# The MLP's second product: its seventh Strassen product by seven inner products as well, and its combined weights made in memory

## The chip, the core and the metric

The kernel runs on one core of a Trainium2 chip. The core has five engines that run side by side, each through its own instructions in order: TensorE (PE in the profile; PEld is its weight load), VectorE (DVE), ScalarE (ACT), GpSimd (POOL) and SyncE (SP, which here only starts transfers). Matmuls write sums into PSUM, which has eight banks of 128 x 512 floats; everything else lives in SBUF, and between SBUF and the device's memory sixteen DMA engines move data. The metric is the time of one execution in microseconds on the device (us). Most executions agree within 0.3 %.

## What is computed

One layer of a diffusion backbone over 1024 tokens of width 1024: a modulated norm, a mixer (pooling beside neighbourhood attention), a residual, a second modulated norm and an MLP with a squared ReLU, a residual again. All that the change touches is the MLP and what follows it:

```python
def _sq_relu_mlp(h, w1, w2):
    return jnp.square(jax.nn.relu(h @ w1)) @ w2
...
        y_x = _sq_relu_mlp(_modulate(x, g_pre_mlp[l], sh2, sc2), w_mlp_in[l], w_mlp_out[l])
        x = x + gt2 * _rmsnorm(y_x, g_post_mlp[l])
```

h is 1024 x 1024, w1 1024 x 4096, w2 4096 x 1024, all in float32. Each operand of a product is split into a high and a low part, and a product is three matmuls (`three`, L220): high by high, high by low, low by high.

## The kernel before

**The second product.** The hidden matrix R (1024 x 4096) by w2 is done by Strassen's method in Winograd's form. R has blocks A11, A12, A21, A22 of 512 tokens by 2048, w2 has blocks b11, b12, b21, b22 of 2048 by 512. Instead of eight block products there are seven: P1 = A11·b11, P2 = A12·b21, a third one S4·b22, P6 = S2·t2, P5 = S1·t1, P7 = S3·t3, P4 = A22·t4. The S are sums of blocks of R, the t sums of blocks of w2; sums and differences of the products give the four blocks of the output. The S are made in `combine_hidden` and `combine_last` (L1981 to L1991) while the first product makes R; R and S go out to memory (`kept`) and come back as operands (`hidden`).

**Groups.** A product with 2048 inner rows is cut into eight groups g of 256 rows (`group`, L2234). A group has 24 matmuls of 512 columns: four tiles t of 128 tokens, each with a PSUM bank of its own, by two blocks of 128 rows by three parts. The four banks of P1 and P2 are called pyx, of P6 pyy, of P5 pyz, of P7 and P4 pyv. The third product is itself done by seven inner products, M1 to M7 (`INNER`, L2119), each of 256 x 1024 by 1024 x 256, in two halves h (`inner_group`, L2310): a half has 24 matmuls of 256 columns, and an inner product has one bank, called pyi. `inner_kept` adds a finished bank into pages c0, c1 (the third product), t and u. So there are 14 inner groups, placed among the groups of P1 and P2.

**Who prepares.** `items` lists all groups in PE's order. At the start of each group, `prepare` (L2169) makes the operands of the item three places further (`AHEAD`): SP loads the hidden block (hrA, hrS) and the weights (b, t), ACT writes the high parts (t_5h, hhA_5h), VectorE the low parts (t_5l, hhA_5l; L175). The weights' parts lie in eight buffers, two to an item, so that those of an item wait until the matmuls of the item four places before are done. In a P6 group `operands` also makes the combined weights on VectorE: t1 = b12 − b11, t2 = t1 − b22, t3 = b22 − b12 (L2095 to L2098), writes t3 out to memory, and adds b21 to t2's page by a transfer of POOL that adds what it brings (`add_to`, L210), which makes t4.

**The order.** Within the last part of the kernel PE, ACT, VectorE and SP run in the order in which the code is written. PE's order there is P1 and P2 with the M groups, P6 and P5 in turn, P7, P4. P4's last four groups are written out another way (`late`): all four for token tile t = 0, then for t = 1, 2 and 3, so that each tile's end work (`finish`) can go on under the next tile's matmuls. In this late part a tile's bank is first made whole by VectorE: L2381 adds u2 into the banks v[t] (pyv) after P4's fourth group.

**The end of rows.** With u2 = P6 + P1 and u4 = P5 + u2, the output halves are: row t < 4, left x[t] (P1 + P2) and right c12 = third product + u4; row 4 + t, right P7 + u4 and left P7 + P4 + u2. `gated` (L2247) squares a half on ACT for the norm and multiplies it by the gate on VectorE (L2251); `finish` (L2270) does this for the second half and computes the norm's root (vy on VectorE L161, ry on POOL); `end` (L2257) multiplies by the root and adds the residual (xo, L2259), and writes the row out. In P7's groups 0 to 3 stand u4 (L2367) and c12 (L2368), in its groups 1 to 4 `finish` of rows 0 to 3, and after P7 the right halves of rows 4 to 7 (L2374).

**The first product.** It is done in 16 pairs of column blocks (`block_pair`, L1999), on the banks phx, phy, phz, phv, with w1's weights wa loaded by SP; from the eleventh pair on (`EARLY`) each pair also loads pages wmb of the modulation's weights, which VectorE sums into accb (L246). In a pair, c22 comes from the bank phv (L2020). Attention runs before, in units i = 0 to 31 (218 to 314 us); there the DMA engines have least to do.

Of the kernel before, what the change touches and what calls it, by code (L numbers as in the profile page):

```python
# [18 lines left out]
P = 128  # L19
# [84 lines left out]
def hybrid_block(ctx, tc, x, ctx_in, w_mod, mod_pages, w_u, b_mod, gp1, gp2, w_in, pool_w, rpb, w_out, w1, w2, vectors,  # L104
# [1073 lines left out]

    with (
# [128 lines left out]
        N = len(units)  # L1308

# [80 lines left out]
        with in_order(ET.PE, ET.Activation, ET.DVE, ET.SP) as projected:  # L1390
# [32 lines left out]
            for i in range(N):  # L1423
# [33 lines left out]
                if i == 2:  # L1457
                    column_sums("sc", accs["sc"], lambda name: pa[:, :256])
# [7 lines left out]
                if 1 < i < N - 1:  # L1466
# [94 lines left out]
    with tc.tile_pool(name="ps2", bufs=6, space=PSUM) as ps2:  # L1561

      def bank(name):
          if (name[:3] in ("phv", "pyi") or name in ("poz_0", "poz_1") or name[:2] == "px" and name[-2:] in ("_3", "_7")
                  or name in ("pyy_3", "pyv_3", "pyz_3")):
              return lasting(name)
          return ps2.tile([P, 512], F32, tag="mm", name=name)

      with ExitStack() as tmp2:
# [257 lines left out]
        def second_steps(b12, b22):  # L1827
# [13 lines left out]
            for name in ("T2", "T1", "T3", "B22", "T4"):  # L1841
# [9 lines left out]
                for n in ("A11", "A12", "A22", "S1", "S2", "S3")}  # L1851
        hidq = [dram.tile([P, 4, 1024], F32, tag=f"hq{h}", name=f"hq{h}") for h in range(2)]
# [49 lines left out]
        def kept(name, p):  # L1902
            if name == "S4":
                return hidq[p // 8][:, p // 2 % 4, (p % 2) * 512 : (p % 2) * 512 + 512]
# [76 lines left out]
        def combine_hidden(p, r11, r21, r22, sa, sb):  # L1981
            nc.vector.tensor_tensor(sa[:, :512], r21, r22, add)
            nc.vector.tensor_tensor(sb[:, :512], r11, r21, sub)
            nc.vector.tensor_tensor(sa[:, 512:], sa[:, :512], r11, sub)  # L1984
# [14 lines left out]
        def block_pair(p, ahead, final=False):  # L1999
# [23 lines left out]
            defer(keep, "A22", p, c22)  # L2023
            if p >= EARLY:
# [34 lines left out]
        w2v = w2.rearrange("(k i p) n -> i p k n", i=2, p=P)  # L2059
        t1, t2 = {}, {}  # L2060
# [22 lines left out]
        def operands(name, g, made=None):  # L2083
            made = made or high_low
            if name == "P1":
                t1[g] = columns(page(f"b11_{g}"), 0, 0, g)
                return hidden("A11", g, g <= AHEAD + 1), made(f"b11_{g}", t1[g])
            if name == "P2":
                return hidden("A12", g), made(f"b21_{g}", wcols("b21", 1, 0, g))
            if name in INNER:  # L2090
                return inner_operands(name, g)
            if name == "P6":

                b12, b22 = wcols("b12", 0, 1, g), wcols("b22", 1, 1, g)
                nc.vector.tensor_tensor(t1[g], b12, t1[g], sub)  # L2095
                t2[g] = page(f"t2_{g}")
                nc.vector.tensor_tensor(t2[g], t1[g], b22, sub)
                nc.vector.tensor_tensor(b12, b22, b12, sub)  # L2098
                nc.gpsimd.dma_start(t3d[g], b12)  # L2099
                parts = hidden("S2", g), high_low(f"t2_{g}", t2[g], -1.0)  # L2100
                if g < NG - 2:
                    last_added(g)
                return parts
            if name == "P5":
                return hidden("S1", g), made(f"t1_{g}", t1[g])
            if name == "P7":
                r = wraw.tile([P, 1024], F32, tag="raw", name=f"t3_{g}")
                nc.sync.dma_start(r, t3d[g])
                if g in (2, 3):
                    last_added(NG - 4 + g)  # L2110
                return hidden("S3", g), made(f"t3_{g}", r)
            return hidden("A22", g), made(f"t4_{g}", t2.pop(g))

        t3d = [dram.tile([P, 1024], F32, tag=f"t3_{g}", name=f"t3_{g}") for g in range(NG)]

        def last_added(g):
            add_to(t2[g].rearrange("p (a f) -> p a f", a=2), w2v[1][:, 2 * g : 2 * g + 2, :512])

        INNER = ("M1", "M5", "M6", "M4", "M2", "M3", "M7")  # L2119
        kept_raw, combine = {}, nc.vector.tensor_tensor  # L2120

        def inner_raw(name, left, r, c, h, at=None):
            if at is None:
                at = tmp.tile([P, 1024], F32, tag="h", name=name, bufs=4) if left else wraw.tile([P, 1024], F32, tag="raw", name=name)
            nc.sync.dma_start(at.rearrange("p (a f) -> p a f", a=4),
                              hidq[h][:, :, c * 512 + r * 256 : c * 512 + r * 256 + 256] if left else
# [315 lines left out]
```

## Time and profile before

| | us |
|---|---|
| median of 3 runs | 1017.34 (1017.3 to 1017.37) |
| the profiled execution | 1017.39 |
| its span in the trace | 1015.6 |
| first product of the second matrix starts (pyx) | 706.9 |
| P6 and P5 start | 835.3 |
| P7 starts | 922.3 |
| P4 starts | 965.9 |

A view of the profile called a timeline has one row for each instruction: start, duration, engine, line, operation, out<-in, and in brackets how long the engine had sat idle before it and what it waited for. Windows give each engine's busy time in a stretch, and the share of the sixteen DMA engines that is taken. Durations overlap a little on a pipelined engine (a matmul of 0.39 us is followed by the next after 0.23), so costs are taken from start to start.

### The profile page before, as it was taken

How to read it: one execution, taken by the hardware profiler on the slowest of the kernel's cores; microseconds unless marked ns; L12 is line 12 of the kernel's file. 1: busy time of each engine (PE TensorE's matmuls, PEld its weight loads, DVE VectorE, ACT ScalarE, POOL GpSimd, SP SyncE). 2: the span in 40 equal slices, each digit the busy share in tenths (PEclk: the TensorE clock that was granted, in tenths of full speed). 3: DMA queues.
4: the chain of work that ended last, by engine and by line, in shares of the span. 5: the costliest groups of instructions: out<-in, count | busy, mean ns of one | idle time of the engine just before them, and what ended most of it. 6: DMA issues, size and time to landing. Idle time of an engine off the chain costs nothing.

```text
span 1015.6 us, 16654 instructions
## 1 busy us (share of the span) xinstructions
PE 1005.2 (99%) x6154; PEld 839.0 (83%) x6154; DVE 772.8 (76%) x1197; ACT 558.8 (55%) x974; POOL 172.4 (17%) x254
## 2 busy tenths in 40 slices
PE   8999999999999999999999999999999999999997
PEld 5788888878998888888888888888889888888886
DVE  5588766968885789879988887755787899757763
ACT  6672254448886746786555554555555454333441
POOL 4111110166774221410000000000000011200200
PEclk9999999999999999999999999999999999999999
DMA  9899798641339945885786656536987799986532
GB/s 362 323 287 315 252 256 306 211 104 43 95 91 224 240 163 178 299 215 195 257 264 204 216 196 223 189 129 241 331 272 235 232 329 292 342 265 237 198 125 84
DMA packets 126722, 229.04 MB, mean 226 GB/s; under 512 B 9712, under 2 KB 61808, under 8 KB 126640
## 3 DMA queue, kind: packets, MB, share of 16 engines
q1 hardware_dynamic: 96240, 166.95, 48.5%
q0 software_dynamic: 13264, 30.06, 13.3%
q10 hardware_dynamic: 17136, 30.97, 8.2%
q8 instruction: 48, 0.79, 0.3%
q14 instruction: 34, 0.28, 0.1%
HBM read 170.25 MB, written 56.64 MB: 223 GB/s over the span
## 4 chain that ended last, share of the span: by engine, by line
PE 96%; DMA 2%; ACT 1%; DVE 0%; SPq 0%; issue 0%; POOL 0%; DVEq 0%; ACTq 0%
PE pu L476 4%; PE pa L1295 4%; PE S L1208 3%; PE phx L221 3%; PE pyx L221 3%; PE phz L221 3%; PE phv L221 3%; PE pyx L222 3%; PE phx L222 3%; PE phv L222 3%; PE phz L222 3%; PE phx L223 3%; PE pyx L223 3%; PE phz L223 3%; PE phv L223 3%; PE pyv L223 3%
## 5 line engine op out<-in xcount | busy, mean ns | idle before, releaser
L1899 ACT ACTIVATE c<-c 128x512 f32<-128x512 f32 x48 | 30.3, 632 | 45.8 <-DVE c L2021 27.2
L1239 ACT ACTIVATE sp<-sp,nm 128x640 f32<-128x640 f32 (+1 forms) x64 | 51.5, 804 | 6.3 <-DVE ri L1243 5.2
L1228 DVE CUSTOM_DVE_ANT_0 sp<-S,tab 128x640 f32<-128x640 f32 (+1 forms) x56 | 44.6, 796 | 13.1 <-PE pz L1261 11.3
L169 ACT CAST wpS<-S 128x512 fp32r<-128x512 f32 x64 | 38.7, 616 | 27.6 <-PE phv L223 10.1
L221 PE MATMUL phx<-thB,wpA 128*128 128x512 f32 x128 | 50.2, 392 | 0.0
L223 PE MATMUL phx<-thB,wpA 128*128 128x512 f32 x128 | 49.8, 389 | 0.0
L222 PE MATMUL phx<-tlB,wpA 128*128 128x512 f32 x128 | 49.8, 389 | 0.0
L175 DVE TENSOR_TENSOR wpS<-S,wpS 128x512 fp32r<-128x512 f32 x64 | 43.5, 687 | 8.0 <-ACT wpS L169 8.0
L1900 ACT ACTIVATE c<-c 128x512 f32<-128x512 f32 x48 | 30.3, 631 | 14.9 <-DVE sa L1984 12.1
L2099 POOL DMA_DIRECT2D t<-b x8 | 4.7, 583 | 144.6 <-DVE b L2098 144.6
L221 PEld LDWEIGHTS phx<-thB,wpA 128*128 128x128 f32 x128 | 24.0, 188 | 5.5 <-ACT s L1952 0.4
L223 PEld LDWEIGHTS phx<-thB,wpA 128*128 128x128 f32 x128 | 24.0, 188 | 5.1
L222 PEld LDWEIGHTS phx<-tlB,wpA 128*128 128x128 f32 x128 | 24.0, 188 | 4.9
L1295 PE MATMUL pa<-pt,v 128*64 128x128 f32 x352 | 25.8, 279 | 0.0
L238 POOL MEMSET accb<- 128x1024 f32 x1 | 1.0, 958 | 142.1 <-ACT c L1900 142.1
L221 PE MATMUL phz<-thB,wpS 128*128 128x512 f32 x64 | 25.0, 391 | 0.0
L221 PE MATMUL phv<-thT,wpA 128*128 128x512 f32 x64 | 25.0, 391 | 0.0
L223 PE MATMUL phz<-thB,wpS 128*128 128x512 f32 x64 | 24.9, 389 | 0.0
L223 PE MATMUL phv<-thT,wpA 128*128 128x512 f32 x64 | 24.9, 389 | 0.0
L222 PE MATMUL phv<-tlT,wpA 128*128 128x512 f32 x64 | 24.9, 389 | 0.0
L221 PE MATMUL phy<-thT,wpS 128*128 128x512 f32 x64 | 24.9, 389 | 0.0
L222 PE MATMUL phy<-tlT,wpS 128*128 128x512 f32 x64 | 24.9, 389 | 0.0
(1216 smaller groups left out, 3572.7 us busy)
## 6 DMA issues: line engine op xcount, KB each, us to landing
b<-in_w SPq DMA_DIRECT2D x32, 512.0 KB, 6.5
hrA<-hdA SPq DMA_DIRECT2D x24, 512.0 KB, 6.5
hrS<-hdS SPq DMA_DIRECT2D x24, 512.0 KB, 6.9
wm<-in_mod_pages SPq DMA_DIRECT2D x16, 512.0 KB, 9.4
wa_0w<-in_w SPq DMA_DIRECT2D x16, 512.0 KB, 4.8
wa_1w<-in_w SPq DMA_DIRECT2D x16, 512.0 KB, 4.2
hdA<-c ACTq DMA_DIRECT2D x32, 256.0 KB, 2.2
hdS<-sa ACTq DMA_DIRECT2D x32, 256.0 KB, 2.2
```

What stands on the lines that cost most here:

```text
L169: nc.scalar.copy(hi, src)
L175: nc.vector.tensor_tensor(lo, src, hi.bitcast(F32), sub)
L221: nc.tensor.matmul(ps, ahi, bhi, start=first, stop=False, skip_group_check=more)
L222: nc.tensor.matmul(ps, ahi, blo, start=False, stop=False, skip_group_check=more)
L223: nc.tensor.matmul(ps, alo, bhi, start=False, stop=last, skip_group_check=more)
L476: nc.tensor.matmul(pus[b][j], wk(wgt, k, low, j * P, P), r, start=(k == 0 and n == 0), stop=(k == KT - 1 and n == 2))
L1208: nc.tensor.matmul(S[e][:, c0 : c0 + k[0].shape[1]], q[n_q][hs, cols], k[n_k][hs], start=(n_q + n_k == 0), stop=(n_q == 1))
L1228: nc.vector.tensor_tensor_reduce(out=to, in0=s, in1=bt, scale=1.0, scalar=BIG, op0=add, op1=ALU.min, accum_out=nm)
L1239: nc.scalar.activation(sp, sp, AF.Exp, bias=least[i, e], scale=-1.0, accum_out=sums[i][:, e : e + 1])
L1295: nc.tensor.matmul(pa[e * HD : (e + 1) * HD, cols], v[:, f : f + HD], turns[i][:, e, c] if c < 4 else fifths[i][:, :, (e + 1) * HD : (e + ...
L1899: nc.scalar.activation(r, src, AF.Relu)
L1900: nc.scalar.activation(r, r, AF.Square)
```

## The change

**P7 becomes seven inner products.** `items` drops P7's eight groups; in their place fourteen inner groups N1 to N7, two halves each, stand one behind each group of P6 and P5 but for the last of either. P6's eight groups now come first, then P5's. `inner_kept` keeps the N sums in pages of their own, which together are c22 in the end part (not to be confused with the pair's c22).

**The combined weights are made in memory.** During the attention units 6 to 29, SP copies blocks of w2 within the device's memory, 24 copies of 512 KB: b22 into the places of t3 and t2, b12 into that of t1 (`block_copied`). In the pairs 2 to 14 of the first product POOL starts 24 adding transfers (`block_sums`): one in pairs 2 and 3, two in each later pair, behind a tiny copy from the pair's c22 ("pace") that keeps POOL from running ahead. POOL now runs in the written order there and to the end. In P6 and P5 the weights are then only loaded, and VectorE's three combinations are gone; t4's adding transfer moves to P5's preparation. The signs of some S are turned to fit.

**The end part.** With P7's groups gone, its work is written around P4's first four groups. u4 stands before them; in P4's group g stand c12 −= u4, `finish` of row g − 1, u2 −= c22, row 4 + g = c22 − u4, and from g = 2 on the gate of row 2 + g. After the additions into v[t] come `finish` of row 3 and the preparation of P4's last group.

The core of the diff:

```diff
+        block_copies = [(to, i, g) for g in range(4) for to, i in ((t3_page, 1), (t1_page, 0), (t2_page, 1))]
...
+        def block_copied():
+            to, i, g = block_copies.pop(0)
+            nc.sync.dma_start(to(g), w2_block(i, 1, g))
...
+                if 5 < i < 30:
+                    block_copied()
...
+        block_sums = [f for g in range(8) for f in (lambda g=g: add_to(t3_page(g), w2_block(0, 1, g)),
+                                                    lambda g=g: add_to(t1_page(g), w2_block(0, 0, g)),
+                                                    lambda g=g: add_to(t2_page(g), t1_page(g)))]
+
+        def block_summed(src, n):
+            if n:
+                pace = sm("pace_" + str(len(block_sums)), 1, 2)
+                nc.gpsimd.tensor_copy(pace, src[:, :1])
+            for _ in range(n):
+                block_sums.pop(0)()
...
             defer(keep, "A22", p, c22)
+            block_summed(c22, 0 if p < 2 or final else 1 if p < 4 else 2)
...
-                b12, b22 = wcols("b12", 0, 1, g), wcols("b22", 1, 1, g)
-                nc.vector.tensor_tensor(t1[g], b12, t1[g], sub)
                 t2[g] = page(f"t2_{g}")
-                nc.vector.tensor_tensor(t2[g], t1[g], b22, sub)
-                nc.vector.tensor_tensor(b12, b22, b12, sub)
-                nc.gpsimd.dma_start(t3d[g], b12)
-                parts = hidden("S2", g), high_low(f"t2_{g}", t2[g], -1.0)
-                if g < NG - 2:
-                    last_added(g)
+                nc.sync.dma_start(two_rows(t2[g]), t2_page(g))
+                return hidden("S2", g), high_low(f"t2_{g}", t2[g])
+            if name == "P5":
+                r = wraw.tile([P, 1024], F32, tag="raw", name=f"t1_{g}")
+                nc.sync.dma_start(two_rows(r), t1_page(g))
+                parts = hidden("S1", g), high_low(f"t1_{g}", r)
+                pace = sm(f"pace_t{g}", 1, 2)
+                nc.gpsimd.tensor_copy(pace, r[:, :1])
+                add_to(two_rows(t2[g]), w2_block(1, 0, g))
                 return parts
...
-        items += [(n, g) for g in range(NG) for n in ("P6", "P5")]
-        items += [(n, g) for n in ("P7", "P4") for g in range(NG)]
+        inner = iter([("N" + n, h) for n in INNER for h in range(2)])
+        for n in ("P6", "P5"):
+            for g in range(NG):
+                items += [(n, g), *islice(inner, 1 if g < NG - 1 else 0)]
+        assert next(inner, None) is None
+        items += [("P4", g) for g in range(NG)]
...
-            for g in range(NG):
-                group(v, "P7", g)
-                if g < 4:
-                    residual(g)
-                    nc.vector.tensor_tensor(u4[g], z[g], u2[g], add)
-                    nc.vector.tensor_tensor(c12[g], c12[g], u4[g], add)
-                if 0 < g < 5:
-                    finish(g - 1, 1, c12[g - 1], xts[g - 1])
-            end()
-            for t in range(4):
-                rows[4 + t] = page(f"row{4 + t}")
-                nc.vector.tensor_tensor(half(4 + t, 1), v[t], u4[t], add)
-            for g in range(NG // 2):
-                group(v, "P4", g, more=True, last=(g == NG // 2 - 1))
-                gated(4 + g, 1, half(4 + g, 1))
+            v, u4, c22 = four("pyv"), halves("u4"), whole("N")
+            for t in range(4):
+                residual(t)
+                nc.vector.tensor_tensor(u4[t], z[t], u2[t], add)
+            for g in range(NG // 2):
+                group(v, "P4", g, last=(g == NG // 2 - 1))
+                nc.vector.tensor_tensor(c12[g], c12[g], u4[g], sub)
+                if g > 0:
+                    finish(g - 1, 1, c12[g - 1], xts[g - 1])
+                rows[4 + g] = page(f"row{4 + g}")
+                nc.vector.tensor_tensor(u2[g], u2[g], c22[g], sub)
+                nc.vector.tensor_tensor(half(4 + g, 1), c22[g], u4[g], sub)
+                if g > 1:
+                    gated(2 + g, 1, half(2 + g, 1))
...
+            finish(3, 1, c12[3], xts[3])
             while coming:
                 prepare()
+            end()
+            for t in (2, 3):
+                gated(4 + t, 1, half(4 + t, 1))
```

What stands in a row on VectorE in P4's groups 2 and 3, up to the first addition into a bank of the late part, before (t and hhA are the low parts of weights and hidden blocks; row the right halves; pyv the bank, u the page of u2):

```order
L175 TENSOR_TENSOR t_5l<-t_5_9543,t_5h 128x1024
L2251 TENSOR_TENSOR row_10230<-row_10230,Gb 128x512
L175 TENSOR_TENSOR hhA_6l<-hrA_6_10345,hhA_6h 128x1024
L175 TENSOR_TENSOR t_6l<-t_6_9621,t_6h 128x1024
L2251 TENSOR_TENSOR row_10232<-row_10232,Gb 128x512
L2381 TENSOR_TENSOR pyv_9885<-pyv_9885,u_9842 128x512
```

and at the same place in the changed kernel, from the low part hhA_6l on (c1Mi holds c12's lower tiles, c1Ni the new c22's, s_8632 is u2's page):

```order
L175 TENSOR_TENSOR hhA_6l<-hrA_6_10622,hhA_6h 128x1024
L175 TENSOR_TENSOR t_6l<-t_6_9665,t_6h 128x1024
L2397 TENSOR_TENSOR c1Mi<-c1Mi,u_10475 128x512
L2281 SCALAR_TENSOR_TENSOR xo_10479<-c_9310,ry_10613,xo_10479 128x512
L2281 SCALAR_TENSOR_TENSOR xo_10479<-c0Mi,ry_10613,xo_10479 128x512
L161 SCALAR_TENSOR_TENSOR vy_10662<-sy_8164,sy_8165 128x1
L2271 TENSOR_TENSOR c1Mi<-c1Mi,Gb 128x512
L2401 TENSOR_TENSOR s_8632<-s_8632,c1Ni 128x512
L2402 TENSOR_TENSOR row_10667<-c1Ni,u_10475 128x512
L2271 TENSOR_TENSOR row_10568<-row_10568,Gb 128x512
L2408 TENSOR_TENSOR pyv_10470<-pyv_10470,s_8631 128x512
```

Between t_6l and the addition into the bank stood one gate; now seven 512-wide operations on data in SBUF, two of them halves of xo, and the little vy stand there. Between t_5l and hhA_6l, where one gate stood, the same list stands once more (c12, two halves of xo, vy, gate, u2, row, gate).

After that addition, VectorE's order up to the last low part, t_7l, is in the changed kernel:

```order
L2408 TENSOR_TENSOR pyv_10471<-pyv_10471,s_8631 128x512
L2408 TENSOR_TENSOR pyv_10472<-pyv_10472,s_8632 128x512
L2408 TENSOR_TENSOR pyv_10473<-pyv_10473,s_8632 128x256
L2409 TENSOR_TENSOR pyw<-pyv_10473,s_8632 128x256
L2281 SCALAR_TENSOR_TENSOR xo_10482<-c_9311,ry_10664,xo_10482 128x512
L2281 SCALAR_TENSOR_TENSOR xo_10482<-c1Mi,ry_10664,xo_10482 128x512
L161 SCALAR_TENSOR_TENSOR vy_10684<-sy_8164,sy_8165 128x1
L2271 TENSOR_TENSOR c1Mi<-c1Mi,Gb 128x512
L175 TENSOR_TENSOR hhA_7l<-hrA_7_10689,hhA_7h 128x1024
L175 TENSOR_TENSOR t_7l<-t_7_9739,t_7h 128x1024
```

Before, hhA_7l followed directly on the addition into pyw; now `finish` of row 3 (xo, vy, gate) stands between.

On POOL, around the eleventh pair of the first product, the changed kernel has the adding transfers (t2d, t3q, t1d are the places of t2, t3 and t1 in memory; c_10 is the eleventh pair's c22):

```order
L238 MEMSET accb 128x1024
L239 DMA accb<-in_b_mod 1x16x64
L2016 COPY pace_7255<-c_10_7225 128x1
L211 DMA t2d_2096<-t1d_2088 128x1024
L211 DMA t3q_2101<-in_w 128x2x512
L2016 COPY pace_7423<-c_11_7393 128x1
L211 DMA t1d_2089<-in_w 128x2x512
L211 DMA t2d_2097<-t1d_2089 128x1024
```

Before, nothing of POOL stood there but the first two rows: the two transfers behind each pace are new.

More of the change, by code (lines that the diff above doesn't have):

```diff
@@ L2055, in block_pair @@
             defer(combine_last, p, c21, sa, sb)
[L2059 to L2060 removed]
+        t2 = {}
         def columns(raw, i, h, g):
@@ L2158, in hybrid_block @@
         AHEAD = 3
-        inner = iter([(n, h) for n in INNER for h in range(2)])
+        inner = iter([("M" + n, h) for n in INNER for h in range(2)])
         items = [("P1", g) for g in range(4)]
@@ L2211, in hybrid_block @@
         fixed.append(True)
-        with tc.issue_after(first[ET.PE]), in_order(ET.PE, ET.Activation, ET.DVE, ET.SP):
+        with tc.issue_after(first[ET.PE]), in_order(ET.PE, ET.Activation, ET.DVE, ET.SP, ET.Pool):
             block_pair(NPAIR - 1, prepare, final=True)
@@ L2258, in end @@
                 for m, rs, xt in ending:
-                    nc.vector.scalar_tensor_tensor(xt, rows[m], rs, xt, mul, add)
+                    parts = [(half(m, h), xt[:, h * 512 : (h + 1) * 512]) for h in range(2)] if m < 4 else [(rows[m], xt)]
+                    for row, to in parts:
+                        nc.vector.scalar_tensor_tensor(to, row, rs, to, mul, add)
                     (nc.gpsimd if m < 4 else nc.sync).dma_start(og[m], xt)
@@ L2322, in inner_group, with whole @@
                     inner_kept(name, ps)
+            def whole(k):
+                return [parts[f"c{t // 2}{k}"][:, t % 2 * 512 : t % 2 * 512 + 512] for t in range(4)]
             x = four("pyx")
             for name, g in items[: items.index(("P6", 0))]:
-                if name in INNER:
+                if name[0] == "M":
                     inner_group(name, g)
@@ L2342, in hybrid_block @@
                         G2 = gate_page("b")
+            c12, left = whole("M"), halves("c11")
             for t in range(4):
-                rows[t] = page(f"row{t}")
+                halves_of_rows[t, 0], halves_of_rows[t, 1] = left[t], c12[t]
                 gated(t, 0, x[t])
-            y, z = four("pyy"), four("pyz")
-            for g in range(NG):
-                group(y, "P6", g)
-                if g == NG - 1:
-                    u2 = halves("u2")
-                    for t in range(4):
-                        nc.vector.tensor_tensor(u2[t], y[t], s1[t], add)
-                group(z, "P5", g)
+            y, z, u2 = four("pyy"), None, s1
+            for name, g in items[items.index(("P6", 0)) : items.index(("P4", 0))]:
+                if name[0] == "N":
+                    inner_group(name, g)
+                elif name == "P6":
+                    group(y, "P6", g)
+                    if g == NG - 1:
+                        for t in range(4):
+                            nc.vector.tensor_tensor(u2[t], s1[t], y[t], sub)
+                        z = four("pyz")
+                else:
+                    group(z, "P5", g)
             xts = {}
```

100 lines of the change are left out of this document (48 added, 52 removed).

## The prediction

> **What bounds the kernel now.** I read the page first, then the timelines of TensorE and VectorE around the products that the change touches, then the loads.
>
> ```profile
> span 1015.6 us, 16654 instructions
> ...
> PE 1005.2 (99%) x6154; PEld 839.0 (83%) x6154; DVE 772.8 (76%) x1197; ACT 558.8 (55%) x974; POOL 172.4 (17%) x254
> ...
> PEclk9999999999999999999999999999999999999999
> DMA  9899798641339945885786656536987799986532
> ...
> PE 96%; DMA 2%; ACT 1%; DVE 0%; SPq 0%; issue 0%; POOL 0%; DVEq 0%; ACTq 0%
> ```
>
> TensorE (PE) is busy 99 % of the span, the chain that ended last is 96 % PE, and the granted clock is in its top tenth in every slice. So the time is the sum of the matmuls, and an edit can act in two ways only: it shortens that sum, or it makes PE wait where it does not wait now. The profiled execution took 1017.39 us, 1.79 us more than its span; the median of the runs is 1017.34, so the sum below, made against 1017.39, can be read against the median as it stands.
>
> **What the change takes from PE.** P7's eight groups of 24 matmuls with 512 columns go; fourteen inner groups of 24 matmuls with 256 columns come. Both kinds stand in the trace (in a timeline row: start us, us, engine, line, operation, out<-in):
>
> ```profile
> 768.58 0.40 PE L221 MATMUL pyx<-b_0h,hhA_0h 128*128 128x512 f32 x1
> ...
> 774.05 0.28 PE L221 MATMUL pyiM<-wM_0h,hhM_0h 128*128 128x256 f32 x1
> ...
> 776.92 0.40 PE L221 MATMUL pyx<-b_1h,hhA_1h 128*128 128x512 f32 x1
> ...
> 927.79 0.39 PE L221 MATMUL pyv<-t_1h,hhS_1h 128*128 128x512 f32 x1
> ...
> 933.23 0.39 PE L221 MATMUL pyv<-t_2h,hhS_2h 128*128 128x512 f32 x1
> ```
>
> A P7 group takes 933.23 − 927.79 = 5.44 us (0.2267 a matmul); eight take 43.5. An inner group, from 774.05 to 776.92, takes 2.87; by the pair of slots, 776.92 − 768.58 − 5.44 = 2.90, and fourteen take 40.6. **PE saves 43.52 − 40.60 = 2.92 us.** This term is nearly sure: the same instructions ran in the same form.
>
> **What the change puts in the tail.** Before, the work that follows P7 and P5 on VectorE (u4, c12, the four rows of `finish`) was spread over P7's eight groups. Now P7 is gone as a stretch of its own, and u4, c12, `finish`, and two new subtractions per group (u2 −= c22, row = c22 − u4) all stand in P4's first four groups, between the low parts that P4 itself needs. VectorE runs in the written order, so I add up what stands there. Prices of the operations:
>
> ```profile
> 930.71 0.69 DVE L2368 TENSOR_TENSOR c0i<-c0i,u 128x512 f32<-128x512 f32 x1
> 931.32 0.15 DVE L161 SCALAR_TENSOR_TENSOR vy<-sy,sy 128x1 f32<-128x1 f32 x1
> 931.39 0.69 DVE L2251 TENSOR_TENSOR row<-c0i,Gb 128x512 f32<-128x512 f32 x1
> ...
> 936.75 1.28 DVE L2259 SCALAR_TENSOR_TENSOR xo<-row,ry,xo 128x1024 f32<-128x1024 f32 x1
> 937.95 0.15 DVE L161 SCALAR_TENSOR_TENSOR vy<-sy,sy 128x1 f32<-128x1 f32 x1
> ```
>
> From start to start a 512-wide addition costs 0.61 us, the little vy 0.07, xo 1.20. Xo now comes as two halves of 512; no row shows such a half, so I bound it by half of 1.20 (0.60) and by the 0.69 of a 512-wide row, and take 0.635. And what stands in P4 today:
>
> ```profile
> 972.37 1.23 DVE L175 TENSOR_TENSOR t_4l<-t,t_4h 128x1024 fp32r<-128x1024 f32 x1 [1.60 <-ACT t_4h L169]
> ...
> 977.81 1.23 DVE L175 TENSOR_TENSOR t_5l<-t,t_5h 128x1024 fp32r<-128x1024 f32 x1 [2.48 <-ACT t_5h L169]
> 978.95 0.69 DVE L2251 TENSOR_TENSOR row<-row,Gb 128x512 f32<-128x512 f32 x1
> 979.55 1.22 DVE L175 TENSOR_TENSOR hhA_6l<-hrA,hhA_6h 128x1024 fp32r<-128x1024 f32 x1
> 980.69 1.22 DVE L175 TENSOR_TENSOR t_6l<-t,t_6h 128x1024 fp32r<-128x1024 f32 x1
> ...
> 983.75 0.70 DVE L2381 TENSOR_TENSOR pyv<-pyv,u 128x512 f32<-128x512 f32 x1 [1.24 <-PE pyv L223]
> ...
> 987.83 0.43 DVE L2381 TENSOR_TENSOR pyv<-pyv,u 128x256 f32<-128x256 f32 x1 [0.66 <-PE pyv L223]
> 988.30 0.43 DVE L2382 TENSOR_TENSOR pyw<-pyv,u 128x256 f32<-128x256 f32 x1
> 988.64 1.22 DVE L175 TENSOR_TENSOR hhA_7l<-hrA,hhA_7h 128x1024 fp32r<-128x1024 f32 x1
> 989.77 1.22 DVE L175 TENSOR_TENSOR t_7l<-t,t_7h 128x1024 fp32r<-128x1024 f32 x1
> ```
>
> and PE's side of it:
>
> ```profile
> 965.87 0.39 PE L221 MATMUL pyv<-t_0h,hhA_0h 128*128 128x512 f32 x1
> ...
> 987.63 0.39 PE L221 MATMUL pyv<-t_4h,hhA_4h 128*128 128x512 f32 x1
> ...
> 991.93 0.39 PE L222 MATMUL pyv<-t_7l,hhA_7h 128*128 128x512 f32 x1
> ```
>
> P4 starts at T = 965.87, its first half ends 21.76 us later, at 987.63, and there PE goes on into the late products of t = 0, which first need VectorE's addition into that bank (v[0], L2381, L2408 after). Before, that addition is done at 984.45, more than 3 us early. After, t_5l can't start earlier than T + 11.94 (it waits for ACT's t_5h, which waits for a buffer that PE frees). Behind it the order of the changed kernel has, up to and with the addition for t = 0: three low parts (3 × 1.14 = 3.42), ten 512-wide operations (c12, gate row, u2, row, gate, twice: 6.05 at 0.605), four halves of xo (2.54), two vy (0.14), and the addition from PSUM (0.70): **12.85 us**, with 987.63 − 977.81 = 9.82 us of PE's work to hide in. **First wait: about 3.05 us.** What stands ahead of t_5l does not add to it: t_4l too waits for ACT, until 972.37 (T + 6.50); behind it come 1.14 of its own, c12, vy, gate, u2 and row of group 1 (2.5) and hhA_5l (1.14), done at T + 11.3, 0.65 us before t_5l can start.
>
> **Second wait.** After the addition for t = 0 stand: those for t = 1, 2 (1.26), two halves (0.81), xo (1.27), vy and gate (0.67), hhA_7l (1.14), t_7l (1.23): 6.4 us, less a tenth for the overlap of neighbours, so t_7l is done 6.3 us after that addition. PE, released by the addition, reaches t_7l after 991.93 − 987.63 = 4.30 us. **Second wait: about 2.0 us**; before, t_7l ended at 990.99, 0.94 us ahead of need. Behind it PE runs to the end as now. The tail costs 3.05 + 2.0 = 5.05 us, with bounds of 0 (all of it slides under PE) and 6.5 (a tenth more for each operation, from the row widths instead of the pitches).
>
> **What making the weights costs elsewhere.** Twenty-four plain copies of 512 KB run under attention; the DMA row above has 0.1 to 0.4 there (ninth to twelfth slice, 203 to 305 us), so I take nothing (if the copies crowded the loads behind attention, it would show as a wait of PE there). Twenty-four adding transfers run beside the MLP's first product, two to a pair of columns from the fifth pair on. Where the pairs from the eleventh on load gate weights as well, there is little room:
>
> ```profile
> 616.04 0.38 SPq L201 DMA_DIRECT2D wa_1w<-in_w  x1
> ```
> ```profile
> 623.70 0.69 DVE L1872 TENSOR_TENSOR S<-wa_0w,wa_1w 128x512 f32<-128x512 f32 x1 [3.95 <-DMA wa_1w<-in_w]
> ...
> 626.84 0.68 DVE L2020 TENSOR_TENSOR c<-phv,c 128x512 f32<-128x512 f32 x1
> ```
> ```profile
> 628.03 0.39 PE L221 MATMUL phv<-thT,wpA 128*128 128x512 f32 x1
> ```
>
> VectorE idled 3.95 us for that load (7.6 us after its issue); four operations later it read the bank phv until 627.52, and PE took that bank again at 628.03: 0.51 us of margin. What an adding transfer costs and how full the queues are (windows: us, PE busy, PEld, DVE, ACT, POOL, clock, DMA share, GB/s):
>
> ```profile
> 608.00:616.00 8.00, 8.00 (x37) 6.62 (x36) 7.76 (x11) 4.77 (x10) 0.00 (x0) 1.00 0.75 238
> 616.00:624.00 8.00, 8.00 (x37) 6.62 (x36) 4.00 (x7) 2.76 (x5) 0.00 (x0) 1.00 0.91 322
> 800.00:838.00 38.00, 38.00 (x222) 33.73 (x221) 34.90 (x33) 19.54 (x26) 3.00 (x4) 1.00 0.94 311
> 838.00:880.00 42.00, 42.00 (x187) 34.76 (x186) 35.19 (x33) 17.57 (x19) 7.78 (x9) 1.00 1.02 319
> ```
> ```profile
> q0 software_dynamic: 1794, 4.69, 43.0%
> ...
> b<-in_w SPq DMA_DIRECT2D x8, 512.0 KB, 10.1
> ...
> t<-in_w POOLq DMA_DIRECT2D x5, 512.0 KB, 9.2
> ```
>
> In 838 to 880 nine transfers of POOL's queue q0, five of them adding, took 43 % of 42 us: 2.0 us of all sixteen engines each. From 608 to 624 the share is 0.83, or 13.3 us of work in 16; two adding transfers make it 17.3, so the load lands 1.3 us late, and 0.51 of that is covered: **about 0.85 us of waiting**, once. Bounds: 0 (the adds land in the free tenth behind), and 4.5 (from 838 to 880 SP's loads of b took 10.1 us at a share of 1.02; a stall of a microsecond in each of the four or five pairs with gate weights).
>
> The Trainium skill ("DMA: Bandwidth & Descriptors", section "Issuing engines are not separate DMA queues") says that transfers issued by SP, ACT and GpSimd run on the same sixteen engines and interleave; the rows agree (1.02 and 10.1 us beside POOL's adds). If they did not share, this term would be 0 and the sum 1019.5.
>
> The stretch of P6, P5 and the new inner groups gets the density of today's P1, P2 with M groups, where PE never waited (800 to 838: 38.00 of 38.00). I take 0. VectorE loses the three combinations of each P6 group and gains the sums of the inner ones; it is not late there. The cover is thin in DMA (0.94), and if it went, each late load would cost about the 0.4 to 1 us by which it missed.
>
> **The sum.** 1017.39 − 2.92 + 3.05 + 2.0 + 0.85 = **1020.4 us**, 0.3 % slower.
>
> **Rivals.**
> - *The tail alone.* The adding transfers hide; the tail is late as worked out: 1017.39 − 2.92 + 5.05 = 1019.5. For it: the free 0.09 to 0.25 of the queues; against it: only 0.51 us of margin. 0.20.
> - *Loads late in several places.* The adds in pairs 11 to 15, and in inner groups with up to four loads of 512 KB in one slot, cost 2 to 4.5 us in place of 0.85: 1021.5 to 1024. For it: a share of 1.02 before; against it: the 38.00 of 38.00 at 0.94. 0.12.
> - *The tail fits: faster.* If VectorE gets through the stretch behind t_5l in 9.8 us in place of 12.85, the addition for t = 0 comes in time, and PE keeps its gain: 1014.5. It decides at a pitch 24 % below the rows' (or t_5l that much earlier); VectorE's idle 2.48 us before t_5l speaks for some slack, but it lies ahead of t_5l, and the stretch that decides lies behind. 0.10.
> - *Half of it.* One wait appears, the other is covered (the 0.94 us of margin, rows at their shortest): near 1017. 0.07.
> - *The clock falls in the first wait.* In the whole span PE is idle for 10.4 us (1015.6 − 1005.2), in many pieces, and the clock stands. If a wait of 3.05 us lowered the granted clock to half for as long again, the matmuls in that stretch would lose 1.5 us: 1022. The trace bears it out weakly, since the clock's row never falls: 0.06. The Trainium skill ("TensorE: Matmul & The Clock Gate", section "What's actually happening") has a free-running window of about 3.4 us after which an idle PE is halved; this trace, which shows no fall, can't say, and 3.05 us lies just below that window.
> - The forecast itself: 0.45. That the change does not do what it says has nothing for it in the orders: the 144 added matmuls and the adding transfers stand there.
>
> **Range and chances.** A difference under 0.2 % (2 us: 1015.3 to 1019.4) is about what a measurement of this kernel can't tell from none. Faster: only the tail that fits, 0.10. Same: half of the tail alone, and the half-covered case: 0.17. Slower: the rest, 0.73. The range 1015.5 to 1024.5 leaves out the fitting tail and the worst of the loads, less than 0.2.
>
> **What would show it.** In the profile of after: (1) inner groups N at 2.9 us a slot, P7's rows gone, PE's busy time lower by about 2.9; (2) VectorE without a gap from t_5l to the addition L2408, and PE waiting there for about 3 us, released by DVE; (3) a wait of about 2 us before the first matmul with t_7l, released by DVE; (4) a wait of PE near 628 us behind wa_1w. A tail without waits, or VectorE idle between P4's low parts, would prove me wrong; so would waits of PE among P6, P5 and the inner groups of more than 1 us.

## The result, and the profile after

The changed kernel took **1041.5 us** (median of 4 runs, 1040.4 to 1042.6), against 1017.3 before: a ratio of 1.0238 (95 % interval 1.0221 to 1.0256). It is 2.4 % slower, eight times the loss that was forecast. Its profiled execution took 1041.15 us, 1039.4 of them span. The first rows of its page:

```profile
span 1039.4 us, 17089 instructions
...
PE 1009.9 (97%) x6298; PEld 846.1 (81%) x6298; DVE 783.2 (75%) x1216; ACT 571.9 (55%) x988; POOL 205.5 (20%) x291
...
DMA  9798897637899945868899988777996695699933
...
q0 software_dynamic: 17616, 38.45, 19.7%
...
PE 81%; DMA 8%; DVE 5%; issue 2%; ACT 2%; POOL 1%; SPq 0%; ACTq 0%; DVEq 0%; POOLq 0%
```

The chain that ended last was 96 % PE; now it is 81 %, and DMA, VectorE, "issue" and ScalarE hold 17. PE's busy time should have fallen by 2.9 us and rose by 4.7: some matmuls got longer, as will be seen. The view of PE's waits (what waited for what, us in total, times, longest) names the places:

```profile
PE phv L221 <- DVE c L2047: 9.8, 4, 3.6
PE phz L221 <- ACT c L2043: 4.4, 3, 1.5
PE pyv L221 <- DVE pyv L2408: 3.6, 1, 3.6
PE pa L1268 <- POOL rb L1252: 1.6, 1, 1.6
```

phv and phz are banks of the first product: 14.2 us of waiting where the forecast had 0.85. Where the span went is read from the first matmuls of each stage (min/median/max duration in ns, then first and last start):

```profile
L221 PE MATMUL pyx<-b_0h,hhA_0h x16: 389/389/396, 727.6 to 794.0; 128*128 128x512 f32 x16
```
```profile
L221 PE MATMUL pyy<-t_0h,hhS_0h x8: 389/389/389, 856.0 to 860.7; 128*128 128x512 f32 x8
```
```profile
L221 PE MATMUL pyv<-t_0h,hhA_0h x8: 389/389/389, 983.6 to 988.4; 128*128 128x512 f32 x8
```

| stretch | before | after | difference |
|---|---|---|---|
| to the start of P1 (attention, first product) | 706.9 | 727.6 | +20.7 |
| P1, P2 with the M groups | 128.4 | 128.4 | 0 |
| P6, P5 and the seventh product | 130.5 | 127.6 | −2.9 |
| P4 to the end | 49.7 | 55.8 | +6.1 |

The seventh product gave just what was worked out. The end part lost 6.1 us where 5.05 stood. Everything else lies ahead of P1, mostly from 546 to 690 us, in the pairs that have the adding transfers beside them.

How one of these waits comes about, first on VectorE, then on PE (timelines):

```profile
610.83 1.28 DVE L246 SCALAR_TENSOR_TENSOR accb<-wmb_0w,sx,accb 128x1024 f32<-128x1024 f32 x1 [8.84 <-DMA accb<-in_b_mod]
```
```profile
617.57 0.79 PE L221 MATMUL phv<-thT,wpA 128*128 128x512 f32 x1 [3.63 <-DVE c L2047]
618.16 0.63 PE L222 MATMUL phv<-tlT,wpA 128*128 128x512 f32 x1
618.58 0.63 PE L223 MATMUL phv<-thT,wpA 128*128 128x512 f32 x1
...
621.38 0.39 PE L222 MATMUL phv<-tlT,wpA 128*128 128x512 f32 x1
```

VectorE stood 8.84 us for a load of 4 KB (the modulation's bias), which POOL had issued behind two adding transfers; its order is fixed, so the reading of phv came late, and PE waited 3.63 us. Then the matmuls start 0.42 us apart in place of 0.23 for nearly 3 us: the granted clock has fallen (0.50 from 617.6 to 620.6 us, windows). From 538 to 706 us the share of the DMA engines rose from 0.58 to 0.85 (windows). And what each adding transfer did to the loads shows in the DMA view of 540 to 700 us (median us from issue to landing last):

```profile
q0 software_dynamic: 4160, 9.44, 37.5%
...
hdS<-sa ACTq DMA_DIRECT2D x18, 256.0 KB, 6.5
...
wa_1w<-in_w SPq DMA_DIRECT2D x7, 512.0 KB, 7.4
```

Before, these two took 2.2 and 4.3 us (540 to 690 us). Seventeen adding transfers were issued in these 160 us, and their queue moved 9.44 MB, which is eighteen times 512 KB. It took 37.5 % of the sixteen engines, 60 us: **3.3 us each** (3.4 by the whole span, see the copying run), not the 2.0 of the forecast.

### The profile page after: what moved, and what is told of

Read it like the earlier page. It is cut to its first block, busy times and chain, and to the rows that moved or that the text cites. A ratio compares the mean times of both kernels' runs of the same rounds, so it can differ in the third digit from the quotient of the medians.

```text
span 1039.4 us, 17089 instructions
## 1 busy us (share of the span) xinstructions
PE 1009.9 (97%) x6298; PEld 846.1 (81%) x6298; DVE 783.2 (75%) x1216; ACT 571.9 (55%) x988; POOL 205.5 (20%) x291
## 3 DMA queue, kind: packets, MB, share of 16 engines
q0 software_dynamic: 17616, 38.45, 19.7%
## 4 chain that ended last, share of the span: by engine, by line
PE 81%; DMA 8%; DVE 5%; issue 2%; ACT 2%; POOL 1%; SPq 0%; ACTq 0%; DVEq 0%; POOLq 0%
PE pu L476 4%; PE pa L1302 3%; PE S L1215 3%; PE pyx L221 3%; PE pyx L222 3%; PE pyx L223 3%; PE phx L221 2%; PE phx L222 2%; PE phx L223 2%; DMA wa_1w<-in_w 2%; PE pyy L221 1%; PE pyz L221 1%; PE pyz L222 1%; PE pyy L222 1%; PE pv L221 1%
## 5 line engine op out<-in xcount | busy, mean ns | idle before, releaser
L2016 POOL COPY pace<-c 128x1 f32<-128x1 f32 x13 | 4.3, 328 | 209.6 <-ACT c L1916 209.6
L2127 POOL COPY pace_t<-t 128x1 f32<-128x1 f32 x8 | 5.1, 639 | 203.5 <-DMA t<-t1d 203.5
L221 PE MATMUL phv<-thT,wpA 128*128 128x512 f32 x64 | 26.9, 420 | 9.8 <-DVE c L2047 9.8
L1888 DVE TENSOR_TENSOR S<-wa_0w,wa_1w 128x512 f32<-128x512 f32 x16 | 11.0, 689 | 26.2 <-issue 17.1
L223 PE MATMUL phv<-thT,wpA 128*128 128x512 f32 x64 | 25.9, 405 | 0.0
L222 PE MATMUL phz<-tlB,wpS 128*128 128x512 f32 x64 | 25.0, 390 | 0.0
```

The source lines that it names most:

```text
L221: nc.tensor.matmul(ps, ahi, bhi, start=first, stop=False, skip_group_check=more)
L222: nc.tensor.matmul(ps, ahi, blo, start=False, stop=False, skip_group_check=more)
L223: nc.tensor.matmul(ps, alo, bhi, start=False, stop=last, skip_group_check=more)
```

## Experiments

Theory A: the adding transfers are the whole loss ahead of P1, because two of them want nearly 7 us of the DMA engines in a pair that has less to spare. Rivals: S3's new place or the order of the pairs; one late load only (the bias); the mere bytes. Apart from that, the end part: is VectorE's queue all of it?

**No adding transfers.**

```diff
             for _ in range(n):
-                block_sums.pop(0)()
+                block_sums.pop(0)
```

> The 24 adding transfers beside the first product are left out (the combined weights then lack their second block); copies, orders and the end part stay. Theory A (the adding transfers fill the DMA engines and every load and store of the pairs lands late): the waits of TensorE on phv and phz between 546 and 690 us vanish, 14 us of waits and 5 us of lowered clock with them; 1041.2 - 19.4 = about 1022, and only the 1.2 us in attention and the 6 us at the end remain. Rival B (the new place of S3 in rows of 2 KB strides, or the order that the scheduler chose for the pairs, makes the pairs late): the waits stay, at least 10 of 14 us, and the time stays above 1035.

1020.1 us. No wait is left from attention to P4 but 0.4 us in attention:

```profile
PE pyv L221 <- DVE pyv L2408: 3.6, 1, 3.6
PE pm L368 <- POOL ident masks.py:199: 1.6, 1, 1.6
...
PE pa L1268 <- POOL rb L1252: 0.4, 1, 0.4
```

P1 starts at 706.5 us (before: 706.9). Theory A holds, and S3's place and the pairs' order cost nothing.

**The bias earlier.**

```diff
         with in_order(ET.Pool):
+            acc_b.append(next(row_b))
             for p in range(1, NPAIR - 1):
```

> The small load of the modulation's bias (4 KB, GpSimd's queue) is issued before the first adding transfer, not behind those of the tenth pair; nothing else moves. If the first long wait (3.6 us at 614 us, and 1.7 us of halved clock behind it) comes from that load, which took 10.6 us to land behind two adding transfers: about 5.3 us less, 1036, and VectorE's 8.8 us before its first addition into accb is gone. If all loads of that pair are simply late, the wait only moves to the next load, wa or wmb: less than 2 us gained, 1039 to 1041.

1046.6 us: nothing gained, rather lost. The wait only moved to the next loads:

```profile
619.66 1.28 DVE L246 SCALAR_TENSOR_TENSOR accb<-wmb_4w,sx,accb 128x1024 f32<-128x1024 f32 x1 [7.90 <-DMA wmb_4w<-in_w_mod]
```
```profile
646.82 0.69 DVE L1888 TENSOR_TENSOR S<-wa_0w,wa_1w 128x512 f32<-128x512 f32 x1 [7.67 <-DMA wa_1w<-in_w]
```

The edit moved more than its expectation said: the first step of the sum of the gate weights now stands ahead of the pairs, so every later step and its load come one place earlier as well (wmb_1w is issued at 584.5 us in place of 597.2). With the bias long there, VectorE still stood for 7.9 us, so the bias's load is one way in which a backlog showed, not its cause. (One run; why it came out above the changed kernel's four runs stays open. Its two longest waits, 6.1 and 6.0 us, again lowered the clock.)

**Copying in place of adding.**

```diff
-        block_sums = [f for g in range(8) for f in (lambda g=g: add_to(t3_page(g), w2_block(0, 1, g)),
-                                                    lambda g=g: add_to(t1_page(g), w2_block(0, 0, g)),
-                                                    lambda g=g: add_to(t2_page(g), t1_page(g)))]
+        copy_to = lambda to, more: nc.gpsimd.dma_start(to, more)
+        block_sums = [f for g in range(8) for f in (lambda g=g: copy_to(t3_page(g), w2_block(0, 1, g)),
+                                                    lambda g=g: copy_to(t1_page(g), w2_block(0, 0, g)),
+                                                    lambda g=g: copy_to(t2_page(g), t1_page(g)))]
```

> The 24 transfers of GpSimd's queue stay with the same bytes, places and times, but copy in place of adding (the sums are then left out). If the price lies in the adding (it reads the place that it writes), the queue's work for one transfer falls from about 3.5 us of the sixteen engines to about 2, and more than half of the 19.4 us goes: 1026 to 1031. If the price is that of bytes from memory to memory on this queue, the time stays within 3 us of 1041.

1026.0 us; P1 starts at 710.3. By the start of P1, 17.3 of the 21.1 us that all the transfers cost (727.6 against 706.5) go with the adding; in the whole time it is 15, because this run's end part lost 2.1 us more (one wait of 5.0 us). The DMA view of 540 to 592 us has

```profile
q0 software_dynamic: 1066, 3.85, 25.8%
```

13.4 us for 3.85 MB, the bytes of 7.3 transfers: 1.8 each. The pages of the two runs, without the transfers and with copies, give it over the whole span:

```profile
q0 software_dynamic: 12112, 25.87, 12.2%
```
```profile
q0 software_dynamic: 15568, 38.45, 16.5%
```

The changed kernel's page has 17616 packets, 38.45 MB and 19.7 % (above). The 24 transfers thus take 80.5 us when they add and 44.8 when they copy: 3.4 and 1.9 us each. Adding from memory to memory costs the engines 1.8 times a copy, and it is not the bytes, which are the same. The adds moved in more packets, though (229 each, the copies 144); whether the packets or the adding itself make the price, no run here separates.

**At what rate?** Fourteen adds in pairs 2 to 9 (two a pair from pair 4), none later:

```diff
-            block_summed(c22, 0 if p < 2 or final else 1 if p < 4 else 2)
+            block_summed(c22, 0 if p < 2 or p >= EARLY else 1 if p < 4 else 2)
```

> Of the 24 adding transfers the 14 in pairs 2 to 9 stay (two a pair from the fifth on); the 10 in pairs 10 to 14, which also load the modulation's weights, are left out (the last weights then lack a block). If the price lies where the pairs carry more loads: 3 to 5 us of loss in the first product, 1023 to 1026. If every adding transfer costs alike (19 us for 24): 11 us of loss, 1030 to 1032.

And thirteen adds, one in each pair 2 to 14:

```diff
+            block_summed(c22, 0 if p < 2 or final else 1)
```

> One adding transfer a pair in all pairs 2 to 14 (13 of 24; the other 11 are left out). Nearly as many as in the run with the first ten pairs, but spread. If the rate decides (two to a pair are 7 us of the sixteen engines in 14 to 16): at most 3 us of loss in the first product, all of it in pairs 10 to 13, 1021 to 1024. If the number decides: 10 us, 1030 to 1032. If the pairs with the modulation's weights bear none at all: 6 to 9 us, 1026 to 1030.

1034.6 and 1026.7 us; P1 starts at 721.1 and 712.1. PE's waits of the first, then of the second:

```profile
PE phv L221 <- DVE c L2047: 5.2, 2, 4.8
PE pyv L221 <- DVE pyv L2408: 3.6, 1, 3.6
PE phz L221 <- ACT c L2043: 3.2, 2, 2.5
PE pyv L222 <- DVE t_7l L175: 1.6, 1, 1.6
```
```profile
PE phv L221 <- DVE c L2047: 2.6, 2, 2.3
...
PE phz L221 <- ACT c L2043: 0.8, 1, 0.8
```

Nearly the same number costs 14.2 us at two a pair and 5.2 at one. The first branch of both expectations was too low (3 to 5, at most 3), and the first run lies above its second branch too; but the order of the two is the rate's. By its time the second run fell into the range of its third branch (the pairs with the gate weights bear none), and 3.6 of its 5.2 us do lie in pairs 10 to 15. In the first, the longest wait (4.8 us) comes after the last add: the bias's load took 12.1 us behind the two adds of pair 9, which took 10.5 and 14.8 to land. A backlog outlives the adds that made it.

Pairs 0 to 9 have 13.6 us each, those from 10 on 19.04. The windows of pairs 4 to 9, before and then in the changed kernel (the share of the DMA engines stands next to last):

```profile
511.07:592.67 81.60, 81.60 (x362) 67.57 (x360) 68.59 (x108) 42.90 (x73) 1.51 (x2) 1.00 0.63 211
```
```profile
512.30:597.45 85.15, 82.23 (x361) 67.42 (x360) 67.53 (x109) 42.64 (x74) 14.45 (x20) 1.00 0.99 270
```

A share of 0.63 leaves 5.0 us of a pair free: one add of 3.4 fits, two (6.7) do not. From pair 10 on the mean has room for two (share 0.56 from 593 to 688 us before, 8.4 us of 19.04 free), and yet 11.3 of the 14.2 us of waits stand there. Pair by pair, the share before and two adds together make 1.13, 0.99 and 0.95 in pairs 10, 11 and 12, where PE waited 3.6, 4.0 and 2.9 us, and 0.70 and 0.78 in pairs 13 and 14, where it waited 0.8 us and not at all. The sum tells where waits come, but does not price them: pairs 3 to 5, at 1.1 and more with the adds that they had, saw none yet, and with one add a pair PE still waited 2.3 us in pair 11 (a sum of 0.82), where VectorE stood 2.15 us for wa_1w.

**The end part, with GpSimd's help.** The rows c22 − u4 and their gates on POOL, finish of rows 1 to 3 behind t_7l:

```diff
+                (nc.gpsimd if m > 3 and h else nc.vector).tensor_tensor(half(m, h), src, G2[:, h * 512 : (h + 1) * 512], mul)
...
+                if g < 3:
+                    nc.vector.tensor_tensor(c12[g], c12[g], u4[g], sub)
+                if g == 1:
+                    finish(0, 1, c12[0], xts[0])
...
+                nc.gpsimd.tensor_tensor(half(4 + g, 1), c22[g], u4[g], sub)
```

> Only the end part is changed: in P4's groups 2 and 3 VectorE keeps the low parts, two subtractions u2 and one c12; the rows c22 - u4 and their gates go to GpSimd, finish of rows 1 to 3 goes behind t_7l. By my sum VectorE is then done with the first addition into a bank (L2409) before TensorE needs it: the wait of 3.6 us and the 2 us of halved clock go, 1041.2 - 6 = about 1035. Rival (ScalarE or the loads are what is late there): a wait stays in that place with another releaser, less than 3 us gained.

1036.1 us: 5 gained, which is near the 6 in part by luck, for 1.9 of them lie ahead of P1 (725.7 us), where the edit changes nothing. The end part gained 3.3: the wait is down to 0.5 us, but P4 to the end still takes 52.5 us, 2.8 more than before; 2.0 of these come after PE's last matmul. VectorE's timeline, then POOL's:

```profile
993.68 2.29 DVE L175 TENSOR_TENSOR t_5l<-t,t_5h 128x1024 fp32r<-128x1024 f32 x1 [1.20 <-ACT t_5h L169]
995.89 1.78 DVE L2397 TENSOR_TENSOR s<-s,c1Ni 128x512 f32<-128x512 f32 x1
```
```profile
994.85 2.28 POOL L2271 TENSOR_TENSOR row<-row,Gb 128x512 f32<-128x512 f32 x1
```

While POOL works on its rows, VectorE's low part takes 2.29 us in place of 1.22 and its subtraction 1.78 in place of 0.68, and POOL's own operations stretch too (up to 2.28 us, against 1.29 for a row at 980.78, while VectorE read a bank). In groups 2 and 3 VectorE gave away four operations, 2.4 us, and its four longer ones cost it 4.4: the work handed over came back as longer operations. The Trainium skill ("GPSIMD Engine Reference", section "Specifications") says that GpSimd's way into SBUF is shared with VectorE, with contention when VectorE has two SBUF inputs; these rows agree, and give its price.

**The end part on VectorE alone,** and no adds:

```diff
+                if g < 2:
+                    nc.vector.tensor_tensor(c12[g], c12[g], u4[g], sub)
+                    nc.vector.tensor_tensor(half(4 + g, 1), c22[g], u4[g], sub)
+                if g == 1:
+                    finish(0, 1, c12[0], xts[0])
...
             while coming:
                 prepare()
+            for t in (2, 3):
+                nc.vector.tensor_tensor(half(4 + t, 1), c22[t], u4[t], sub)
+            finish(1, 1, c12[1], xts[1])
...
+            finish(3, 1, c12[3], xts[3])
```

> No adding transfers (as in the run without them, the combined weights lack their second block), and an end part that leaves VectorE room without GpSimd: in P4's groups 2 and 3 only the low parts, u2 and one gate each, and row and c12 of tiles 2 and 3 and finish of rows 1 to 3 behind t_7l. If the waits in the end part come from VectorE's queue alone: no wait of TensorE above 0.3 us there, P4 to the end 49.7 to 50.5 us as before the change, and 1017.3 - 2.9 = 1014.4 to 1015.2 in all. If VectorE is too full whatever the order (its work of about 28 us against 31.6 up to the end): the end moves out, 1016 to 1019.

1016.4 us, 1.0 below the kernel before on the same chip; no wait in the end part, P4 to the end 50.5 us (0.7 more than before). It started a little late: PE waited 1.0 us more than usual for the first activations, within the first 60 us, and 0.4 in attention. The seventh product's gain is there (127.6 us from P6 to P4), and nearly all that the end part lost came back by another order alone.

**Kernels that keep all the sums.** The first spreads the 24 adds: six beside the out projection, twelve in pairs 1 to 9, six beside P2.

```diff
+                block_summed(s5[t], 1)
...
+            block_summed(c22, 0 if p < 1 or p >= EARLY else 2 if p in (2, 4, 6) else 1)
...
+                if block_sums:
+                    block_summed(raw, 1)
```

> A complete kernel: all 24 adding transfers stay but are placed where the queues have room by the windows (six beside the out projection, 357 to 390 us; twelve in pairs 1 to 9, one or two each; none from pair 10 on; six beside P2), the copies start three units later in attention, and the end part leaves VectorE room as in the run above. By the theory that adds cost only where the loads have no room: 1014.5 to 1018. If two to a pair still make the loads late (2 to 4 us in pairs 4, 6): 1018 to 1020. If the places beside the out projection or P2 have no room either: above 1020.

1023.0 us, and unsteady (1019.8 to 1026.5); ratio 1.0060 (1.0037 to 1.0083), slower than the kernel before. In its profile (1020.5) nothing is lost beside the out projection or P2; the waits stand in the pairs again, 2.8 us at 510 us, behind the two adds of pair 2:

```profile
507.92 0.69 DVE L1903 TENSOR_TENSOR S<-wa_0w,wa_1w 128x512 f32<-128x512 f32 x1 [4.52 <-DMA wa_1w<-in_w]
```

The second makes t2 on VectorE again (one addition for a P6 group), which leaves 16 adds, none beside the pairs: seven beside the out projection, eight beside P2, one in P6.

```diff
-                nc.sync.dma_start(two_rows(t2[g]), t2_page(g))
+                nc.sync.dma_start(two_rows(t2[g]), t1_page(g))
+                b22 = wcols("b22", 1, 1, g)
+                nc.vector.tensor_tensor(t2[g], t2[g], b22, add)
```

> A complete kernel: no adding transfer beside the first product at all. t2 is made on VectorE again (t1 + b22, one addition for a P6 group), so that 16 adding transfers and 16 copies are left: seven adds beside the out projection, eight beside P2, one in P6's first group; copies from attention's unit 11 on; the end part of the run without adds. If adds beside the pairs are the whole loss: TensorE has no wait above 0.5 us from attention to the end, P6 to P4 still takes 127.6 us, 1014.6 to 1015.5 us (2 us faster than before). If VectorE's eight additions or the eight more loads in P6's groups are late: waits there of 0.3 to 1 us a group, 1016 to 1021. If the adds beside the out projection or P2 make loads late: waits at 360 to 430 or 770 to 840 us, above 1017.

1016.55 us (1016.2 to 1019.9), ratio 1.0001 (0.9992 to 1.0010): no change. P1 starts at 706.1, as hoped. One wait is left, in P6's first group, where a weight of the inner product came late (its load Ti took some 16 us to land):

```profile
832.00 1.23 DVE L175 TENSOR_TENSOR wN_0l<-Ti,wN_0h 128x1024 fp32r<-128x1024 f32 x1 [4.49 <-ACT wN_0h L169]
...
838.35 2.48 DVE L2278 TENSOR_TENSOR c<-pyx,Gb 128x512 f32<-128x512 f32 x4
```
```profile
839.09 0.50 PE L221 MATMUL pyy<-t_0h,hhS_0h 128*128 128x512 f32 x1 [1.74 <-DVE c L2278]
```

The third thins the places: seven beside the out projection, one each in pairs 2, 5, 8, 13 and 14, four beside P2.

```diff
+            if p in (2, 5, 8, 13, 14):
+                block_summed(c22, 1)
...
+                if g % 2:
+                    block_summed(raw, 1)
```

> As the last kernel (t2 on VectorE, 16 adding transfers), with the places thinned: seven adds beside the out projection, one each in pairs 2, 5, 8, 13 and 14, four beside P2 (every second group). If a single adding transfer of 3.5 us fits into a pair now and then, and the last kernel's wait of 1.7 us in P6's first group came from the eight adds beside P2 (loads of 9 us there): no wait above 0.5 us, 1014.6 to 1015.5 us in all. If any adding transfer in a pair makes a load late: 0.5 to 2.5 us of waits near 500, 545 or 590 us, 1015.5 to 1018. If the wait in P6 comes from VectorE's additions for t2 alone: it stays, 1016 to 1017.

**1014.5 us** (8 runs, 1014.3 to 1014.7) against 1017.3: ratio 0.9973 (0.9962 to 0.9983), 0.3 % faster than the kernel before. Its page has

```profile
span 1012.7 us, 17098 instructions
...
PE 1002.3 (99%) x6298; PEld 843.4 (83%) x6298; DVE 794.7 (78%) x1224; ACT 573.1 (57%) x988; POOL 195.5 (19%) x284
```

PE is busy 2.9 us less than before, and the span is 2.9 us shorter: in sum the whole of the saving arrives. By stretches it is not quite so: P1 starts 0.7 us earlier than before (a lead that is there at 398 us already), and P4 to the end takes 50.5 us, 0.8 more; the two cancel. The five adds in the pairs left no wait of PE there; PE's longest wait is the 1.6 us of its start, as before.

## Why the prediction was wrong

**PE's saving: right.** 2.92 us worked out, 2.9 measured in the changed kernel (130.5 to 127.6) and 2.9 at the end of the study. P6 and P5 with the inner groups took no wait, as priced.

**The term that failed: "about 0.85 us of waiting, once"** for the adding transfers; it was 20.7 us, 1.3 of them already in attention. Two steps of it were wrong.
- *The price.* It took 2.0 us of the engines per transfer from a row that mixed adds into SBUF with plain writes. Adds from memory to memory were in no row of before, and take 3.4; a plain copy takes 1.8 to 1.9. The forecast gave no upper bound for this number, though no row of the trace gave it.
- *The place.* It looked for one wait at one thin margin (0.51 us in the twelfth pair) and added up one stretch of 16 us (its own figures make 1.3 − 0.51 = 0.8 there, not 0.85). The question was one of rate: 6.7 us of adds in pairs of 13.6 us with 5.0 free. There the engines were full (0.99), a backlog went from pair to pair, and all loads and stores beside it slowed down, 4.3 to 7.4 us for wa_1w. Late loads also start the next ones late: SP issued pair 10's wa_0w 1.3 us behind VectorE's first step of accb, at 598.8 us before and at 612.2 after, when that step had stood for the bias. The bound of 4.5 us, one microsecond in each of the pairs with gate weights, had no such growth in it, so the range ended far below the result. The waits in pairs 6 and 7, ahead of the gate weights, were not foreseen at all.

The rule cited with this term, one set of DMA engines under all queues, held (SP's wa_1w and ACT's stores slowed down beside POOL's adds); what was missing was how much an adding transfer takes of them. The rival of loads late in several places named the mechanism with a chance of 0.12 and sizes of 2 to 4.5 us.

**The first wait in the end part: right in place, 3.6 us for 3.05.** t_5l started at P4's start + 11.94 us, exactly as before. Behind it:

```profile
995.57 1.23 DVE L175 TENSOR_TENSOR t_5l<-t,t_5h 128x1024 fp32r<-128x1024 f32 x1 [0.60 <-ACT t_5h L169]
...
1004.53 0.75 DVE L2281 SCALAR_TENSOR_TENSOR xo<-c,ry,xo 128x512 f32<-128x512 f32 x1 [0.46 <-POOL ry L163]
...
1008.34 2.22 DVE L2408 TENSOR_TENSOR pyv<-pyv,s 128x512 f32<-128x512 f32 x4
```

The halves of xo took 0.665 each (0.635 assumed), and one waited 0.46 us for the root from POOL, which the sum did not have.

**The second wait, and the clock rival: they changed places.** The forecast had 2.0 us of waiting for t_7l, and gave a falling clock 0.06, with a loss of 1.5 us. The clock fell:

```profile
1009.17 0.47 PE L221 MATMUL pyv<-t_4h,hhA_4h 128*128 128x512 f32 x1 [3.62 <-DVE pyv L2408]
...
1010.09 0.63 PE L221 MATMUL pyv<-t_4h,hhA_4h 128*128 128x512 f32 x1
1010.52 0.63 PE L222 MATMUL pyv<-t_4l,hhA_4h 128*128 128x512 f32 x1
...
1015.33 0.50 PE L222 MATMUL pyv<-t_7l,hhA_7h 128*128 128x512 f32 x1
```

From 1010.09 the matmuls stand 0.43 us apart, until 1013.1; seven of them lose 0.2 us each, 1.6 us with the edges. That slows PE by about what VectorE was late, so t_7l is just in time. In the run with the first fourteen adds the clock stood behind the same wait, and there the wait for t_7l shows (1.6 us). In these two runs the end part lost 6 us; that it is near the forecast's 5.05 in the changed kernel is in part luck, for the second loss had another cause. It was not always 6: with one add a pair it was 6.9, with copies 8.2, where t_5l itself started 0.8 us later and one more operation waited for a root.

In the first product, 20.7 us less 14.2 of waits and 1.3 in attention leave 5.2. Some 3.5 of them are two falls of the clock, behind the waits of 3.6 and 2.9 us; the rest stands at the waits themselves, whose gaps are some 0.2 us longer from start to start than the idle time shown.

**The copies in attention** were priced at nothing. The share of the DMA engines rose from 0.34 to 0.69 there (203 to 305 us), and PE's wait for POOL's rb rose from nothing to 1.6 us in the changed kernel and 0.4 to 1.0 in others, and vanished where the copies start later. That the copies slow POOL's small transfers there is likely, but no run tried it alone.

## What to carry to other kernels

When transfers move into a stretch, compare a rate with a rate: what they take of the DMA engines in one period of the loop, against what the windows show free there. Above it a backlog grows, and no single margin tells its price; a little below it single loads can still come late. Give an operation that the trace does not have an upper bound before the range is drawn: here an add from memory to memory took 1.7 times what was assumed. And when work loses the stretch that covered it, write it where the waiting engine does not stand behind it: here the same operations in another order gave back 5.3 of the 6.1 us.

## What the hardware showed that I had not expected

- An adding transfer of 512 KB from memory to memory takes 3.4 us of all sixteen DMA engines, a copy of the same 1.9; a 4 KB load queued behind two adds took 10.5 us to land, 2.4 before.
- VectorE's operations on SBUF take up to 2.6 times as long (0.68 to 1.78 us) while GpSimd computes on SBUF as well.
- Behind some waits of PE the granted clock falls to 0.50, and 512-wide matmuls stand 0.43 us apart in place of 0.23, for some 3 us. The length of the wait alone does not decide it. From attention on, over all these runs, no wait of 2.35 us or less did it; those of 2.49, 2.60, 2.81 and 2.93 us did, those of 2.52 and 2.94 did not; of eleven from 3.6 us up, all but one of 3.63 did. The two that contradict a simple threshold, first from the run with fourteen adds, then from the one with GpSimd's help:

```profile
549.55 0.50 PE L221 MATMUL phz<-thB,wpS 128*128 128x512 f32 x1 [2.49 <-ACT c L2043]
...
550.43 0.63 PE L221 MATMUL phz<-thB,wpS 128*128 128x512 f32 x1
550.86 0.63 PE L222 MATMUL phz<-tlB,wpS 128*128 128x512 f32 x1
```
```profile
563.36 0.50 PE L221 MATMUL phz<-thB,wpS 128*128 128x512 f32 x1 [2.94 <-ACT c L2043]
563.69 0.39 PE L222 MATMUL phz<-tlB,wpS 128*128 128x512 f32 x1
563.92 0.40 PE L223 MATMUL phz<-thB,wpS 128*128 128x512 f32 x1
```
